# Decode attention's score and value products put into one stretch per round, the exponentials' transposition ahead of it

## The chip, the cores and the metric

The kernel runs on one core of one Trainium2 chip. The metric is the device time of one execution in microseconds (us). Engines are named as in the profile: PE is TensorE (PEld its weight loads), DVE is VectorE, ACT is ScalarE, POOL is GpSimd, SP is SyncE, which only issues transfers.

## What is computed

One inference step of a hybrid decoder layer, in float32. A prompt of 2048 new tokens and 64 sample tokens (8 sequences of 8 tokens) pass through the same layer; only the sample tokens have a cache of 8192 old tokens per sequence, in pages of 128 tokens.

```python
def diff_attn(q, k, v, q_pos, k_pos, lam):
    s = jnp.einsum('bqhcd,bkhcd->bchqk', q, k, preferred_element_type=jnp.float32) * (D_HEAD ** -0.5)
    dist = q_pos[:, None] - k_pos[None, :]
    bias = -alibi_slopes()[:, None, None] * dist.astype(jnp.float32)[None]
    s = jnp.where((dist >= 0)[None, None, None], s + bias[None, None], NEG)
    p = jax.nn.softmax(s, axis=-1)
    a = p[:, 0] - lam * p[:, 1]
    return jnp.einsum('bhqk,bkhd->bqhd', a.astype(v.dtype), v)

def sample_attention(q, k, v, lam, k_pool, v_pool, page_table):
    ...
    kp = k_pool[page_table].reshape(bd, past, N_HEADS, 2, D_HEAD)
    vp = v_pool[page_table].reshape(bd, past, N_HEADS, D_V)
    k_all = jnp.concatenate([kp.astype(k.dtype), k], axis=1)
    v_all = jnp.concatenate([vp.astype(v.dtype), v], axis=1)
    return diff_attn(q, k_all, v_all, past + jnp.arange(tn), jnp.arange(past + tn), lam)

def block_forward(x, conv_state, attend, ...):
    h = rmsnorm(x, norm1_g)
    b, c, u, q, k, v = project(h, w_in)
    y_conv, new_conv = short_conv(b, c, u, conv_state, conv_w)
    o = rmsnorm(attend(q, k, v, lam), subln_g) * (1.0 - lam_init)
    x = x + jnp.concatenate([y_conv, o], axis=-1) @ w_out
    h2 = rmsnorm(x, norm2_g)
    x = x + jnp.square(jax.nn.relu(h2 @ w_up)) @ w_down
```

There are 4 heads, 2 maps per head, 64 numbers per key and 128 per value. "The decode" below is `sample_attention`; the rest (projections, prompt attention, MLP) is "the dense work".

## The kernel before

The dense work is one long stream of products on PE: input projection, prompt attention, output projection and MLP. Each dense product is split into three (`wh`, `wl` are the high and low part of a weight tile; ACT makes `wh`, DVE makes `wl`), and its moving side is 384 or 512 columns wide.

The decode is a generator, `decode()`, with an inner generator `rounds()`. After every dense group of three products `tick(us)` adds to a credit; when the credit is positive and at least `gap * gs` us (by the kernel's own estimates) have gone by since the last step, the generator runs to its next `yield cost, gap`. So the decode's instructions are strewn among the dense ones at fixed places, decided when the program is made; every engine then runs its own list in order. `gp()` gives the gaps, `GP` for the first two sequences and `GP2` for the others, and `gs` is 0.7.

A round takes 1024 cached tokens of a sequence (a pair of chunks of four pages). A sequence has 8 rounds of scores, and its values come 8 rounds later. So a full round has the scores of sequence b and the values of sequence b-1. There are 64 rounds of scores and 64 of values; 48 rounds have both, 16 only scores, 16 only values. The first two sequences run during the input projection, and the other six after the prompt attention, during the output projection and the MLP. A full round does, in this order:

- Scores (line 902): 16 products `sps<-kt,qbd`, in two halves of 8 (one per map), with a `yield` behind each half. Four heads use four column groups of the array, 32 columns of weights each (column tiling). A float32 product is two instructions in the trace. DVE then adds the bias and takes maxima (line 910).
- Some of the next round's transposed keys on DVE: `more(MO[0])`, that is 5 of 8 transposes (`transpose_k`, line 717), then 2 and 1. After the 4th and the 8th, `gather_k` on POOL fetches another chunk's keys (line 699, 128 rows of 8 KB, `kraw`).
- Exponentials (line 858, ACT) that the next round's values need.
- Transposition of this round's exponentials on PE (`pps`, line 937, 4 full-array products) and their copy by ACT to `ptt` (line 940).
- Values (line 949): two halves `e` of 16 products `o_ps<-vpg,ptt`, 16 columns of weights in each of four column groups, with a `yield` behind each half. A half takes its `vpg` tile, four groups `g` of 128 tokens. Behind each half `gather_v` issues four gathers on POOL (line 707, 128 rows of 2 KB each) for the same half of the next round. There are two `vpg` buffers, so a half's buffer is filled again only when its products are done.

Dense sums have 5 of the 8 PSUM banks, the decode 3. A "stretch" below is an unbroken run of column-tiled products on PE with dense products ahead and behind. The last round of a sequence has some more work (new tokens, normalisation) and dense products around it.

Of the kernel before, what the change touches and what calls it, by code (L numbers as in the profile page):

```python
# [8 lines left out]
F32 = mybir.dt.float32  # L9
# [9 lines left out]
P = 128  # L19
# [47 lines left out]
def tile_hymba_step(  # L67
# [68 lines left out]
    def rsqrt(y, v, n, w, eng=None):  # L136
        """y[:n, :w] = v ** -0.5 by Newton's iteration from the exponent trick."""
# [38 lines left out]
    def between(us):  # L176
        """A place between two products where other work of the tensor engine may go."""
        if fillers:
            fillers.pop(0)()
        else:  # L180
            tick(us)
# [15 lines left out]
    def mm3(ps, wh, wl, ah, al, first, last):  # L197
        """ps += (wh + wl)^T (ah + al), all but the product of the two low parts."""
        nc.tensor.matmul(ps, lhsT=wh, rhs=ah, start=first, stop=False)  # L199
        nc.tensor.matmul(ps, lhsT=wh, rhs=al, start=False, stop=False)  # L200
        nc.tensor.matmul(ps, lhsT=wl, rhs=ah, start=False, stop=last)  # L201

    class Weights:
        """Streams [128, 1024] weight tiles and splits each into two float32r parts, ahead of use."""
# [29 lines left out]
        def parts(self):  # L234
            """Closures that split the next tile, a half at a time."""
# [26 lines left out]
        def ahead(self, n):  # L262
            """Splits the next n tiles after those taken."""
            self.split(self.ng + n)
# [6 lines left out]
    def norm_sum(x, n, junk=None):  # L271
        """The mean square of each row of x[:n]."""
# [6 lines left out]
    def norm_root(ss, n, eng=None):  # L279
        """(ss + EPS) ** -0.5 for one value a row."""  # L280
# [23 lines left out]
    # order of the column groups of w_in: Q, K, V, then (C, U, B) per convolution group  # L304
# [5 lines left out]
    # the last block ends with Q, whose results leave without a transpose  # L310
# [4 lines left out]
    # token tiles of each block in two chunks of columns: (source, first row, rows, column)  # L315
# [28 lines left out]
    def prep_sum(bi, ci, ss, i):  # L344
        """Sums of squares of a tile of tokens."""
        x, n = xt[bi, ci][i], chunks[bi][ci][i][2]
        junk = sb.tile([P, D], BF16, tag="nat", bufs=4, name="junk")
        nc.scalar.activation(junk[:n], x[:n], AF.Square, scale=1.0 / 32.0, accum_out=ss[:n, i:i + 1])
# [14 lines left out]
    def prep_scale(bi, ci, rr):  # L363
        """Closures that normalise a chunk's tokens."""
# [7 lines left out]
    def trans(bi, ci):  # L372
        """Closures that transpose and split a chunk's tokens."""
# [29 lines left out]
    # the first tile's norm by itself  # L403
# [42 lines left out]
    class Proj:  # L446
        """One column group of w_in for one block of tokens."""
# [163 lines left out]
    def proj2(bi, mi):  # L611
        """Two column groups, chunk by chunk: at the ends of a block, where the activations change."""
# [58 lines left out]
    def row_fold(dst, src, op):  # L671
        """dst[(h,g,q), c] = over g: op of src[(h,g,q), c]."""
# [10 lines left out]
    def decode():  # L683
# [28 lines left out]
        def transpose_k(r, t, k):  # L712
            """An eighth of the transposed keys of a pair of chunks."""
# [11 lines left out]
        def load_qc(j):  # L725
            """Queries of four batches."""
# [13 lines left out]
        # page rows: keys in rows of 32 groups of four tokens, values token by token  # L740
# [9 lines left out]
        # bias of a cached key: slope (key - end of its pair of chunks) + slope (that end - query)  # L750
# [31 lines left out]
        # a page's scores and values have token 4 s + j in row 32 j + s  # L782
# [3 lines left out]
        # rows of the scores: (head, page in the group of four, token of the sample)  # L786
# [13 lines left out]
        # lambda on every partition  # L800
# [6 lines left out]
        # rows of the output: (head, map, token) in the first 16 of each 32  # L807
# [7 lines left out]
        # new tokens: column s of group g is token 32 g + s = (batch 4 g + s // 8, s % 8)  # L815
        # distance t - q; allowed where it is not positive
        nc.vector.tensor_scalar(scr[:, 0, :], scr[:, 0, :], rowf[:, 0:1], None, op0=ALU.subtract)
        # owner batch of the column, for this row's group
# [17 lines left out]
        # collects rows (h, c, q) into columns (h, q)  # L836
# [13 lines left out]
        def exps(b, k):  # L850
            """Exponentials of a batch's eighth k of the cached keys; NPR: of the new keys."""
# [8 lines left out]
        def more(n):  # L860
            """Some more of the next pair's transposed keys."""
# [6 lines left out]
        def rounds():  # L868
            """The pairs of chunks of batches b0 to b1."""
# [14 lines left out]
            for r in range(b0 * NPR, N_PR + NPR):  # L884
                b, i = divmod(r, NPR)
                pb = b - 1 if b > b0 else -1
                nk = 0
                if r < N_PR:
# [7 lines left out]
                    # scores of this pair of chunks of four pages  # L896
                    sps = dps.tile([P, 2, 256], F32, tag="sps", bufs=DPB - 1, name="sps")
                    for c in range(2):
# [9 lines left out]
                        yield 1.05, gp()[0] if c else gp()[1]  # L908
                    for c in range(2):
                        nc.vector.tensor_tensor_reduce(  # L910
                            sq[:, c, :], sps[:, c, :], base.rearrange("p e j s -> p (e j s)"), 1.0, -3e38,
                            op0=ALU.add, op1=ALU.max, accum_out=cur["mx"][:, c, i:i + 1])
                    if i == NPR - 1 and r + 1 < N_PR:
# [4 lines left out]
                more(MO[0])  # L918
                if pb >= 0:
                    u = st[pb]  # L920
                    if i < NPR - 1:
                        exps(pb, i + 1)
                    else:
                        m2 = small.tile([P, 2], F32, tag="m2", name="m2")
                        nc.vector.tensor_reduce(m2, u["sm"], axis=AX.X, op=ALU.add)
                        sv = small.tile([P, 2], F32, tag="sv", name="sv")
                        row_fold(sv, m2, ALU.add)
                        nc.vector.reciprocal(sv, sv)
                        wr = dk.tile([P, 1], F32, tag="wr", bufs=2, name="wr")
                        nc.vector.tensor_tensor_reduce(sv, sv, osel, 1.0, 0.0, op0=ALU.mult, op1=ALU.add, accum_out=wr)  # L930
                        u["w"] = wr
                    yield 0.0, gp()[2]
                    more(MO[1])
                    pps = dps.tile([P, 2, 2, P], F32, tag="sps", bufs=DPB - 1, name="pps")
                    for e in range(2):
                        for c in range(2):
                            nc.tensor.transpose(pps[:, e, c, :], u["s"][i][:, c, P * e:P * e + P], ident)
                    ptt = dk.tile([P, 2, 16, 2, 8], F32, tag="ptt", name="ptt")
                    for e in range(2):
                        nc.scalar.copy(ptt[:, e].rearrange("p x c q -> p c x q"),  # L940
                                       pps[:, e].rearrange("p c (x q) -> p c x q", q=8))
                    more(MO[2])
                    yield 0.4, gp()[3]
                    for e in range(2):
# [12 lines left out]
                        more(MO[3 + e])  # L957
                        yield 1.2, gp()[4 + e]
                else:
                    for _ in range(3):  # L960
                        yield 0.0, gp()[6]
                        more(2)
                    yield 0.0, gp()[7]
# [75 lines left out]
        # sub-norm of the sample tokens: sums over the partitions by a product with ones  # L1039
# [59 lines left out]
    # units in groups of about four chunks of keys  # L1099
# [9 lines left out]
    # loads by the iteration after which they are issued  # L1109
# [11 lines left out]
    def attention_first():  # L1121
        """The attention's first tiles, ahead of the input projection's end."""
# [7 lines left out]
        # key - query position for the last query block; masked past the diagonal  # L1130
# [36 lines left out]
    def mlp_weights(nxt):  # L1167
        """In order of use; those of the next tokens' output projection come before the last ones."""
# [19 lines left out]
    class Dense:  # L1188
        """Output projection, MLP and final norm of some tokens.

        groups: lists of tiles (source, result, first row, rows); each group of tiles is one chunk of columns.
        """
# [65 lines left out]
        def turn(self, ti, g):  # L1258
            """Transposes and splits half of a tile's normalised tokens."""
# [12 lines left out]
        def norm_early(self, ti, ss):  # L1272
            """Closures for a tile whose group's products go on; all but two tiles of a group wait for its end."""
# [18 lines left out]
        def product(self, ps, ti, w, k2, ks=None):  # L1292
            """Adds the products of a pair of rows of chunks of w_out."""
# [9 lines left out]
        def out_proj(self):  # L1303
# [18 lines left out]
            for half in range(2):  # L1322
                # the first tiles share each pair of rows of weights as it comes
# [58 lines left out]
        def first_ups(self):  # L1382
            """The first ones, group by group: the last group's activations are still being made."""
# [15 lines left out]
        def down(self, ms, after=None):  # L1399
# [26 lines left out]
            if after is not None:  # L1426
                # the result of the last tile, by halves
# [12 lines left out]
        def final(self, ti, eng, last_too=0):  # L1440
            """Final norm: the statistics of tile ti, the result of the tile before it."""
# [11 lines left out]
        def run(self, ub, poll, before_last, nxt, after):  # L1453
# [11 lines left out]
            if len(self.groups) == 1 and KUP:  # L1465
                # the last ones together, half by half of the rows: the memory then takes other tokens' data
# [685 lines left out]
```

## Time and profile before

| | |
|---|---|
| median of three runs | 3152.28 us (3148.69 to 3154.98) |
| profiled execution, first to last instruction | 3153.6 us |
| PE busy / DVE / ACT / POOL | 96% / 58% / 39% / 28% of the span |
| first stage with decode (input projection) | about 110 to 590 us |
| second stage with decode (output projection, MLP) | about 1240 to 2220 us |

A row of the timeline gives the start, the time from the first start to the last end, the engine, the line, and what is written from what; `x16` means that 16 instructions of one kind stand together. Matmuls overlap, so the pace is read from one start to the next. A bracket gives the engine's idle time before the row, and who ended it.

### The profile page before, as it was taken

The page shows a single profiled execution, that of the slowest core. Times are in us where ns is not written, and L with a number is a line of the kernel's source. Part 1 is how long each engine was busy: PE and PEld are TensorE (multiplying, and loading weights), DVE is VectorE, ACT ScalarE, POOL GpSimd, SP SyncE. Part 2 cuts the span into 40 slices and gives each one's busy share as a digit, 9 for nine tenths or more (in the row PEclk, how much of TensorE's full clock was granted, in tenths as well). Part 3 has the DMA queues.
Part 4 walks back from the last instruction along what each step waited for, and adds up shares of the span by engine and source line. Part 5 has one row for each costly group of instructions (what it writes and reads, how often), then busy time and mean ns, then how long its engine had stood idle before and what let it go on. Part 6 is the DMA issues. An engine that isn't in the chain of part 4 may idle for free. (4 is left out here: it accounts for less than half of the span.)

```text
span 3153.6 us, 53285 instructions
## 1 busy us (share of the span) xinstructions
PE 3014.2 (96%) x20902; PEld 2532.3 (80%) x20902; DVE 1824.8 (58%) x3751; ACT 1243.3 (39%) x2705; POOL 891.8 (28%) x1266
## 2 busy tenths in 40 slices
PE   7999998999999989999999999999999999999998
PEld 7988887989997788777677777777887788888886
DVE  5376353268888668766676776663653444444444
ACT  3323323357778643333343333343332332222222
POOL 0013355211122121455466564467002010000002
PEclk9999999999999999999999999999999999999999
DMA  4777876754335457899689899677741112111111
GB/s 149 229 232 247 286 255 200 223 140 113 108 99 146 139 176 242 278 320 334 229 288 360 304 347 328 211 274 263 230 145 41 61 54 67 47 54 47 54 47 64
DMA packets 400821, 585.80 MB, mean 186 GB/s; under 512 B 35413, under 2 KB 299605, under 8 KB 384186
## 3 DMA queue, kind: packets, MB, share of 16 engines
q1 hardware_dynamic: 337418, 301.07, 31.1%
q0 software_dynamic: 61984, 277.91, 24.5%
q8 instruction: 165, 2.70, 0.3%
q10 hardware_dynamic: 1168, 3.41, 0.3%
q14 instruction: 86, 0.70, 0.1%
HBM read 526.56 MB, written 55.74 MB: 185 GB/s over the span
## 5 line engine op out<-in xcount | busy, mean ns | idle before, releaser
L707 POOL DMA_INDIRECT vpg<-in_cache_v_dram,pt x512 | 537.5, 1050 | 232.3 <-issue 134.4
L226 ACT CAST wh<-wraw 128x1024 fp32r<-128x1024 f32 x336 | 350.0, 1048 | 632.2 <-PE dps L1412 277.1
L228 DVE TENSOR_TENSOR wl<-wraw,wh 128x1024 fp32r<-128x1024 f32 x336 | 410.2, 1221 | 236.4 <-ACT wh L226 227.4
L199 PE MATMUL ups<-h2h,wh 128*128 128x384 f32 (+2 forms) x1264 | 462.6, 366 | 4.9 <-DVE x L1417 2.5
L1417 DVE TENSOR_TENSOR x<-dps,x 128x512 f32<-128x512 f32 (+1 forms) x528 | 355.2, 684 | 177.2 <-PE dps L1412 176.7
L1410 PE MATMUL dps<-wh,uh 128*128 128x512 f32 (+1 forms) x1076 | 438.8, 408 | 13.2 <-ACT wh L226 5.6
L201 PE MATMUL ups<-h2h,wl 128*128 128x384 f32 (+2 forms) x1264 | 448.8, 355 | 0.0
L200 PE MATMUL ups<-h2l,wh 128*128 128x384 f32 (+2 forms) x1264 | 447.9, 354 | 0.0
L1411 PE MATMUL dps<-wl,uh 128*128 128x512 f32 (+1 forms) x1076 | 425.5, 395 | 4.3 <-DVE wl L228 3.3
L1412 PE MATMUL dps<-wh,ul 128*128 128x512 f32 (+1 forms) x1076 | 424.2, 394 | 0.0
L199 PE MATMUL ps<-hh,wh 128*128 128x384 f32 (+1 forms) x1152 | 404.6, 351 | 1.1 <-ACT cc L1526 0.7
L201 PE MATMUL ps<-hh,wl 128*128 128x384 f32 (+1 forms) x1152 | 376.5, 327 | 3.1 <-DVE wl L228 3.1
L200 PE MATMUL ps<-hl,wh 128*128 128x384 f32 (+1 forms) x1152 | 376.0, 326 | 0.1
L1369 DVE TENSOR_TENSOR ul<-r,uh 128x384 fp32r<-128x384 f32 (+2 forms) x158 | 93.6, 592 | 438.5 <-ACT uh L1368 438.3
L717 DVE STREAM_TRANSPOSE kt<-kraw 128x512 f32<-128x512 f32 x512 | 316.9, 678 | 5.4 <-DMA kraw<-in_cache_k_dram,idxk 5.4
L699 POOL DMA_INDIRECT kraw<-in_cache_k_dram,idxk x128 | 129.1, 1009 | 565.6 <-DVE kt L717 522.8
L199 PEld LDWEIGHTS ups<-h2h,wh 128*128 128x128 f32 x1264 | 238.5, 189 | 54.4 <-issue 28.7
L1410 PEld LDWEIGHTS dps<-wh,uh 128*128 128x128 f32 (+1 forms) x1076 | 200.8, 187 | 85.8 <-issue 24.1
L1366 ACT ACTIVATE r<-ups 128x384 f32<-128x384 f32 (+2 forms) x158 | 82.8, 524 | 445.0 <-PE ups L201 445.0
L200 PEld LDWEIGHTS ups<-h2l,wh 128*128 128x128 f32 x1264 | 238.9, 189 | 16.6
L201 PEld LDWEIGHTS ups<-h2h,wl 128*128 128x128 f32 x1264 | 238.5, 189 | 15.3
L284 POOL TENSOR_SCALAR ss<-ss 128x1 f32<-128x1 f32 (+1 forms) x33 | 9.5, 289 | 839.5 <-ACT junk L276 838.7
(275 smaller groups left out, 4985.8 us busy)
## 6 DMA issues: line engine op xcount, KB each, us to landing
wraw<-in_w_up_dram SPq DMA_DIRECT2D x128, 512.0 KB, 5.0
wraw<-in_w_down_dram SPq DMA_DIRECT2D x128, 512.0 KB, 3.3
wraw<-in_w_in_dram SPq DMA_DIRECT2D x72, 512.0 KB, 4.4
wraw<-in_w_out_dram SPq DMA_DIRECT2D x32, 512.0 KB, 4.2
x<-in_x_prompt_dram SPq DMA_DIRECT2D x24, 512.0 KB, 7.0
vpg<-in_cache_v_dram,pt POOLq DMA_INDIRECT x512
qt<-QH SPq DMA_DIRECT2D x64, 128.0 KB, 4.5
qt<-QL SPq DMA_DIRECT2D x64, 128.0 KB, 5.0
```

Of the source, the lines that this page charges most:

```text
L199: nc.tensor.matmul(ps, lhsT=wh, rhs=ah, start=first, stop=False)
L200: nc.tensor.matmul(ps, lhsT=wh, rhs=al, start=False, stop=False)
L201: nc.tensor.matmul(ps, lhsT=wl, rhs=ah, start=False, stop=last)
L226: nc.scalar.copy(wh, t)
L228: eng.tensor_sub(wl, t, wh.bitcast(F32))
L699: nc.gpsimd.indirect_dma_start(out=t.rearrange("p a b -> p (a b)"), out_offset=None, in_=ck, in_offset=bass.IndirectOffsetOnAxis(ap=idxk[: ...
L707: nc.gpsimd.indirect_dma_start(out=t[:, g, :], out_offset=None, in_=cv, in_offset=bass.IndirectOffsetOnAxis(ap=idxv[:, 4 * it + g:4 * it + ...
L717: nc.vector.transpose(t[:, e, 16 * j:16 * j + 16].rearrange("p a b -> p (a b)"), kraw[2 * r + e][:, 16 * j:16 * j + 16].rearrange("p a b - ...
L1410: nc.tensor.matmul(ps, lhsT=uh, rhs=wh[:, half], start=(i == 0), stop=False)
L1411: nc.tensor.matmul(ps, lhsT=uh, rhs=wl[:, half], start=False, stop=False)
L1412: nc.tensor.matmul(ps, lhsT=ul, rhs=wh[:, half], start=False, stop=(i == len(ms) - 1))
L1417: nc.vector.tensor_add(xx, ps, xx)
```

## The change

In `rounds()`, the transposition `pps` and the copies to `ptt` come first in a round, with a `yield` behind them. Then both halves of the scores and both halves of the values are issued without a `yield` between, with all eight gathers of the next values behind their halves; then the first five transposed keys, and one `yield` with the summed cost and the gap `gp()[0] + gp()[1]`. The exponentials for the next round come after that, with two more transposed keys, a `yield` with gap `gp()[2] + gp()[4]`, and the last transposed key. The sum of a full round's gaps falls from 12 to 10 (`GP2`), its `yield`s from six to three. Comments were taken out elsewhere.

```diff
                 nk = 0
+                if pb >= 0:
+                    u = st[pb]
+                    pps = dps.tile([P, 2, 2, P], F32, tag="sps", bufs=DPB - 1, name="pps")
+                    for e in range(2):
+                        for c in range(2):
+                            nc.tensor.transpose(pps[:, e, c, :], u["s"][i][:, c, P * e:P * e + P], ident)
+                    ptt = dk.tile([P, 2, 16, 2, 8], F32, tag="ptt", name="ptt")
+                    for e in range(2):
+                        nc.scalar.copy(ptt[:, e].rearrange("p x c q -> p c x q"),
+                                       pps[:, e].rearrange("p c (x q) -> p c x q", q=8))
+                    yield 0.4, gp()[3]
+                cost = 0.0
                 if r < N_PR:
...
-                        yield 1.05, gp()[0] if c else gp()[1]
                     for c in range(2):
                         nc.vector.tensor_tensor_reduce(
...
+                    cost += 2.1
...
+                if pb >= 0:
+                    for e in range(2):
+                        it = NCH * pb + 2 * i + e
+                        v = vpg.pop(it)
+                        for g in range(4):
+                            for h in range(H):
+                                nc.tensor.matmul(
+                                    o_ps[32 * h:32 * h + 16, :],
...
+                        if it + 2 < b1 * NCH:
+                            gather_v(it + 2)
+                    cost += 2.4
                 more(MO[0])
+                yield cost, gp()[0] + gp()[1]
                 if pb >= 0:
-                    u = st[pb]
                     if i < NPR - 1:
                         exps(pb, i + 1)
...
-                    yield 0.0, gp()[2]
                     more(MO[1])
...
+                    yield 0.0, gp()[2] + gp()[4]
                     more(MO[2])
-                    yield 0.4, gp()[3]
-                    for e in range(2):
...
-                        more(MO[3 + e])
-                        yield 1.2, gp()[4 + e]
                 else:
                     for _ in range(3):
-                        yield 0.0, gp()[6]
                         more(2)
-                    yield 0.0, gp()[7]
+                        yield 0.0, gp()[6]
```

The list of PE in a full round of the MLP stage before, from one transposition to the first dense products behind the second half of the scores (`ups` and `dps` are dense sums):

```order
L937 MATMUL pps<-ident,sq 128x128 x4
...
L949 MATMUL o_ps<-vpg,ptt 16x128 x16
L1410 MATMUL dps<-wh,uh 128x512
...
L949 MATMUL o_ps<-vpg,ptt 16x128 x16
L1410 MATMUL dps<-wh,uh 128x512
...
L902 MATMUL sps<-kt,qbd 32x256 x8
L1410 MATMUL dps<-wh,uh 128x512
...
L902 MATMUL sps<-kt,qbd 32x256 x8
L1410 MATMUL dps<-wh,uh 128x512
```

From this transposition to the next there are 57 dense products, 9 of them between the two halves of the values. The same place in the program after, the lines now 893 (`pps`), 914 (scores) and 937 (values):

```order
L893 MATMUL pps<-ident,sq 128x128 x4
L1413 MATMUL dps<-wh,uh 128x512
...
L1415 MATMUL dps<-wh,ul 128x512
L914 MATMUL sps<-kt,qbd 32x256 x16
L937 MATMUL o_ps<-vpg,ptt 16x128 x32
L1413 MATMUL dps<-wh,uh 128x512
```

The four stretches have become one, with 12 dense products between the transposition and the stretch and 30 from the stretch to the next transposition. Over the whole program the runs of score or value products with dense products between fall from 256 to 80. No dense product is added or removed.

On ACT the same place after reads as follows (`wh<-wraw` is a cast of a weight tile that came by a transfer):

```order
L896 COPY ptt<-pps 128x2x16x8 x2
L226 CAST wh<-wraw 128x1024
L858 ACTIVATE sq,sm<-sq,no 128x256 x2
L226 CAST wh<-wraw 128x1024
L896 COPY ptt<-pps 128x2x16x8 x2
```

The exponentials `sq` of line 858 are read by the transposition whose copy is the last row here; before the change a whole round lay between the two.

## Rows read from the trace of the kernel before

**Rows 1.** The page: busy time and share of each engine, whole span.

```profile
PE 3014.2 (96%) x20902; PEld 2532.3 (80%) x20902; DVE 1824.8 (58%) x3751; ACT 1243.3 (39%) x2705; POOL 891.8 (28%) x1266
```

**Rows 2.** Windows: stretch, length, PE, PEld, DVE, ACT, POOL busy, PEclk, DMA share, GB/s.

```profile
1812.00:1908.00 96.00, 96.00 (x927) 73.87 (x926) 69.48 (x119) 36.78 (x73) 65.25 (x61) 1.00 0.98 351
```

**Rows 3.** Timeline of PE, parts of two full rounds.

```profile
1826.57 0.60 PE L937 MATMUL pps<-ident,sq 128*128 128x128 f32 x4
1826.93 0.48 PE L1410 MATMUL dps<-wh,uh 128*128 128x512 f32 x1
1827.24 0.39 PE L1411 MATMUL dps<-wl,uh 128*128 128x512 f32 x1
...
1829.31 0.39 PE L1411 MATMUL dps<-wl,uh 128*128 128x512 f32 x1
1829.53 0.39 PE L1412 MATMUL dps<-wh,ul 128*128 128x512 f32 x1
1829.85 1.07 PE L949 MATMUL o_ps<-vpg,ptt 128*16 128x128 f32 x32
1830.85 0.50 PE L1410 MATMUL dps<-wh,uh 128*128 128x512 f32 x1
1831.19 0.40 PE L1411 MATMUL dps<-wl,uh 128*128 128x512 f32 x1
...
1838.55 0.34 PE L201 MATMUL ups<-h2h,wl 128*128 128x384 f32 x1
1838.82 1.07 PE L902 MATMUL sps<-kt,qbd 128*32 128x256 f32 x16
1839.82 0.44 PE L199 MATMUL ups<-h2h,wh 128*128 128x384 f32 x1
1840.10 0.34 PE L200 MATMUL ups<-h2l,wh 128*128 128x384 f32 x1
1840.27 0.34 PE L201 MATMUL ups<-h2h,wl 128*128 128x384 f32 x1
```

**Rows 4.** Timeline within that score stretch: its last eight, its last four instructions.

```profile
1839.27 0.61 PE L902 MATMUL sps<-kt,qbd 128*32 128x256 f32 x8
1839.49 0.40 PE L902 MATMUL sps<-kt,qbd 128*32 128x256 f32 x4
```

**Rows 5.** Line 937 in 1811:1910, then in 2117:2206 (values only): count, ns, first and last start.

```profile
L937 PE MATMUL pps<-ident,sq x28: 271/272/273, 1811.6 to 1908.7; 128*128 128x128 f32 x28
...
L937 PE MATMUL pps<-ident,sq x32: 271/272/273, 2118.7 to 2204.7; 128*128 128x128 f32 x32
```

**Rows 6.** POOL's groups in 1812:1908, the last in 1600:1800: count, busy us, mean ns.

```profile
L707 POOL DMA_INDIRECT vpg<-in_cache_v_dram,pt x48 | 52.4, 1092 | 14.6 <-issue 12.2 <-DMA vpg<-in_cache_v_dram,pt 1.2 <-PE dps L1412 0.6
L699 POOL DMA_INDIRECT kraw<-in_cache_k_dram,idxk x12 | 12.6, 1047 | 17.3 <-DVE kt L717 16.1 <-issue 0.9 <-DVE ul L1369 0.3
...
L289 POOL TENSOR_SCALAR ss<-ss 128x1 f32<-128x1 f32 x9 | 7.3, 813 | 1.4 <-DVE ss L287 0.8
```

**Rows 7.** Timelines of PE and POOL, 2148 to 2165: a half of values, three gathers, the wait.

```profile
2148.02 1.07 PE L949 MATMUL o_ps<-vpg,ptt 128*16 128x128 f32 x32
...
2149.39 0.94 POOL L707 DMA_INDIRECT vpg<-in_cache_v_dram,pt  x1 [4.16 <-PE o_ps L949]
...
2159.04 1.89 POOL L707 DMA_INDIRECT vpg<-in_cache_v_dram,pt  x1 [0.30 <-issue]
...
2164.21 0.41 PE L949 MATMUL o_ps<-vpg,ptt 128*16 128x128 f32 x8 [1.58 <-DMA vpg<-in_cache_v_dram,pt]
```

**Rows 8.** PE's waits over the whole span: total us, times, longest.

```profile
PE o_ps L949 <- DMA vpg<-in_cache_v_dram,pt: 20.7, 25, 2.3
...
PE o_ps L949 <- ACT ptt L940: 13.3, 6, 5.0
```

**Rows 9.** Windows around a wait for `vpg`: columns as in group 2.

```profile
2196.00:2200.00 4.00, 2.02 (x36) 1.02 (x35) 0.00 (x0) 0.00 (x0) 3.05 (x4) 1.00 0.98 324
2200.00:2203.50 3.50, 3.50 (x14) 3.50 (x13) 0.48 (x1) 2.04 (x4) 2.62 (x3) 0.53 0.64 224
```

More of the change, by code (lines that the diff above doesn't have):

```diff
@@ L917, in rounds @@
                         gather_v(b0 * NCH + 1)
-                more(MO[0])
                 if pb >= 0:
-                    u = st[pb]
[L921 to L931, printed above, removed]
-                    yield 0.0, gp()[2]
-                    more(MO[1])
-                    pps = dps.tile([P, 2, 2, P], F32, tag="sps", bufs=DPB - 1, name="pps")
-                    for e in range(2):
[L936 to L942, printed above, removed]
-                    yield 0.4, gp()[3]
                     for e in range(2):
@@ L956, in rounds @@
                             gather_v(it + 2)
-                        more(MO[3 + e])
-                        yield 1.2, gp()[4 + e]
+                    cost += 2.4
+                more(MO[0])
+                yield cost, gp()[0] + gp()[1]
+                if pb >= 0:
+                    if i < NPR - 1:
+                        exps(pb, i + 1)
+                    else:
+                        m2 = small.tile([P, 2], F32, tag="m2", name="m2")
+                        nc.vector.tensor_reduce(m2, u["sm"], axis=AX.X, op=ALU.add)
+                        sv = small.tile([P, 2], F32, tag="sv", name="sv")
+                        row_fold(sv, m2, ALU.add)
+                        nc.vector.reciprocal(sv, sv)
+                        wr = dk.tile([P, 1], F32, tag="wr", bufs=2, name="wr")
+                        nc.vector.tensor_tensor_reduce(sv, sv, osel, 1.0, 0.0, op0=ALU.mult, op1=ALU.add, accum_out=wr)
+                        u["w"] = wr
+                    more(MO[1])
+                    yield 0.0, gp()[2] + gp()[4]
+                    more(MO[2])
                 else:
                     for _ in range(3):
+                        more(2)
                         yield 0.0, gp()[6]
-                        more(2)
-                    yield 0.0, gp()[7]
                 if pb >= 0 and i == NPR - 1:
```

## Prediction

> **What bounds the kernel now.** I read the busy line first: PE is busy 96% of the span, no other engine over 58% [rows 1]. So time falls by what PE is spared, unless a new wait takes it back. The window 1812 to 1908 us, with six full rounds, shows what else is near its end there [rows 2]: PE has no idle time in 96.00 us, the DMA share is 0.98 at 351 GB/s, and POOL, whose busy time leaves out the gaps between its issues, is at 65 of 96 us. Rounds stand 16.2 us apart, (1908.7 - 1811.6) / 6 [rows 5]. So in this stage PE is the bound, with DMA and POOL close behind.
>
> **What the change removes.** The timeline gives a stretch's price by comparing starts with the dense pace. Dense products of 512 columns start about 0.23 us apart, those of 384 about 0.17. From the last dense start ahead of a half of the scores to the second one behind it are 1840.10 - 1838.55 = 1.55 us, 1.21 more than two paces; a half of the values costs 1831.19 - 1829.53 - 0.46 = 1.20 [rows 3]. Within a score stretch a group of four column tiles starts every 0.22 us [rows 4], so four groups need 0.88 and the other 0.33 us is entering and leaving the stretch. Values are half as wide, eight groups at half the distance: the same. The order has 256 stretches before and 80 after, so 176 x 0.33 = 58 us go. The step from scores to values inside the new stretch is not in the trace; it costs 0 to 0.33 us in 48 rounds, 0 to 16 us. I take 0, since the groups within a stretch show no break when the head or the weights change. The transpositions cost 0.44 us (1827.24 - 1826.57 - 0.23) before and after, and no product is added.
>
> **What the change moves, PE.** Rounds come closer, since the summed gaps are shorter. In the order after, a full round has 42 dense products where it had 57: 18 of 384 columns and 24 of 512 make 8.6 us, the transpositions 0.44, the stretch 4 x 0.87 + 0.33 = 3.8, together 12.8 us. Worked out so for all, 36 full rounds have an own length of 12.3 to 13.5 us, mean 12.6, and 13 rounds of values alone 10.6 to 12.1, mean 11.3; the others lie further apart (ends of sequences, other dense work in between) and are not in danger. What has to fit into a round besides is unchanged: ten gathers on POOL, 4.2 MB of keys and values (two times 1 MB and eight times 256 KB).
>
> **POOL.** In the window of group 6 six rounds have 48 value gathers of 1.09 us and 12 key gathers of 1.05, and each is followed by a gap of 0.30 us [rows 6, 7]: (52.4 + 12.6 + 60 x 0.30) / 6 = 13.8 us a round. That fitted into 16.2 us, and POOL even waited 16.1 us in the window for transposed keys. It does not fit into 12.6. From 1600 to 1800, some twelve rounds long, POOL has norm work as well, the largest group alone 7.3 us [rows 6]; for this I add 0.6 us a round. So short full rounds take 14.4 us, and PE waits 36 x (14.4 - 12.6) = 65 us.
>
> **The value gathers' chain.** A half's buffer is refilled only behind its own products. A half starts at 2148.02, its first gather at 2149.39, 1.37 us later. A last gather started at 2159.04 lasted 1.89, and PE's fourth group was released at 2164.21, 3.28 us after the gather's end [rows 7]. After the change both halves stand back to back, so eight gathers follow the first half: 1.37 + 8 x 1.39 - 0.30 + 3.28 = 15.5 us until the second half's fourth group may go, which stands 0.87 + 0.65 = 1.5 us into the next round's values. The rounds must be 13.9 us apart (12.8 with undisturbed gathers of 0.95). Before, nine dense products of 0.17 us and another entry lay between the halves, 1.9 us more time for the late half: 12.0, and the trace has (2204.7 - 2118.7) / 7 = 12.3 us in the stage with values alone [rows 5]. So the formula holds. In full rounds POOL's 14.4 covers this; in rounds of values alone PE waits 13 x (13.9 - 11.3) = 34 us. The present waits for `vpg`, 20.7 us [rows 8], are replaced by these.
>
> **What I cost at nothing.** The exponentials are now needed about 3 us (a gap of 4 x 0.7) after their place instead of a round later, behind weight casts on ACT that themselves await transfers; PE's transposition would wait, with all dense products behind it. In return the copies to `ptt` have the scores' 1.75 us as extra cover; PE waits 13.3 us for them now [rows 8]. I take the two as even, -13 to +13. The key gathers stand behind eight value gathers in POOL's list, so keys land later and DVE, which transposes them, holds up sums behind it. DVE is busy 69 of 96 us [rows 2] and dense sums have five banks; without that cover it is perhaps 1 us in 36 rounds, but within a round that waits for POOL anyway. The rounds of scores alone only lose a stretch (counted); their moved key transposes lie under the dense work.
>
> **Sum.** -58 + 65 + 34 - 21 = +20 us. The profiled execution has a span of 3153.6 us against a median of 3152.3, so the sum carries over: 3172 us, 0.6% more.
>
> **The rivals.**
>
> *The gathers keep up (faster).* If POOL's gathers take their undisturbed 0.95 + 0.30 us, ten take 12.5 and with the norm work 13.1; full rounds wait 36 x 0.5 = 18 us, values alone 13 x (12.8 - 11.3) = 20, and the sum is -58 + 38 - 21 = -41: 3111 us. For it: the shorter gathers shown took 0.94 [rows 7]. Against it: the mean in the densest window is 1.09, and denser rounds would not lower it. It decides from short full rounds of under 13.9 us, where the sum is zero.
>
> *DMA is the bound.* A round of 16.2 us at 351 GB/s is 5.7 MB; with 42 instead of 57 dense products' weights 5.3 MB remain, 15.1 us at that rate, and the share was 0.98 [rows 2]. Full rounds then wait 36 x 2.5 = 90 us: +45, 3197 us. Against it: PE did not wait at this share. The Trainium skill ("DMA: Bandwidth & Descriptors", "Where 436 GB/s comes from") puts the HBM limit of a core at about 358 GB/s; by that a round would take 14.8 us and the time be 3186 us, and the window's 351 GB/s agrees with it.
>
> *The clock falls.* Behind a wait of nearly 2 us for `vpg`, PE was granted 0.53 of its clock for 3.5 us (its level of 1.2 GHz), where it had 1.00 before [rows 9]: 1.6 us lost. If every second of the 49 waits brings this and it adds to the sum, it is 24 x 1.6 = 39 us: 3211 us. Against it: POOL works on meanwhile, so a slower PE mostly shortens the next wait. The Trainium skill ("TensorE: Matmul & The Clock Gate", "HAM oscillation — how this bites in real kernels") tells of a kernel that falls to the lower clock at each wait for a transfer; these rows agree that a wait can do it.
>
> **How the numbers follow.** My forecast (rounds of 13.9 to 14.9 us, 3154 to 3190) has 0.53, the gathers that keep up 0.23, DMA 0.14, the clock 0.10. Changes within 0.2%, 6 us, can hardly be told from none: of my forecast's chance 0.14 lies there and 0.03 below. Faster 0.26, same 0.14, slower 0.60. The range 3112 to 3212 reaches from the second case, half of which it leaves out, to the fourth; it holds the unknown 16 and 13 us.
>
> **What the profile after would show.** Stretches of about 3.8 us, and PE's instructions otherwise unchanged: the 58 us. PE's wait for `vpg` from 20.7 to about 100 us, at the last groups of the second half. Short full rounds 14 to 15 us apart, with POOL's issues nearly without a pause; rounds of values alone about 14. Wrong if short rounds come at 13 us (then faster), if PE waits for weights (DMA), for `sq` or for `kt`, or if the granted clock falls under 0.95 between 1300 and 2200 us.

## The result, and the profile after

The changed kernel takes 3264.56 us (median of four runs, 3255.69 to 3270.32) where the kernel before takes 3153.35 beside it: 1.0356 times as long, 95% interval 1.0335 to 1.0378, 111 us more. The direction was forecast, the size was not: 3172 us, and 3212 as the end of the range.

The page of the changed kernel (lines 893 `pps`, 896 `ptt`, 914 scores, 937 values, 699 and 707 the gathers, 717 the key transposes): the busy line, and the chain that ended last.

```profile
PE 3001.7 (92%) x20902; PEld 2594.0 (80%) x20902; DVE 1821.5 (56%) x3751; ACT 1245.0 (38%) x2705; POOL 890.8 (27%) x1266
...
PE 52%; DMA 16%; issue 13%; DVE 8%; POOL 8%; ACT 3%; SPq 0%; POOLq 0%; ACTq 0%; DVEq 0%
DMA kraw<-in_cache_k_dram,idxk 7%; DMA vpg<-in_cache_v_dram,pt 6%; PE ups L199 5%; PE ups L201 5%; PE ups L200 5%; PE dps L1414 5%; PE dps L1415 5%; PE dps L1413 5%; POOL vpg L707 5%; PE asc L1835 4%; PE O L1922 3%; PE ps L199 3%; PE ps L201 3%; PE ps L200 3%; DVE kt L717 2%
...
L717 DVE STREAM_TRANSPOSE kt<-kraw 128x512 f32<-128x512 f32 x512 | 326.9, 684 | 184.9 <-DMA kraw<-in_cache_k_dram,idxk 184.4
```

PE is busy only 12.5 us less than in [rows 1], and not because little was saved. Its mean granted clock fell from 0.986 to 0.968 over the span. The clock has two levels in these traces, full and half. Before, it was at half for 86 us, and PE was busy in 77 of them; after, for 206 us, with PE busy in 163. Counting a busy us at half clock as half a us of work, the clock costs half of that busy time: 38 us before, 81 after. Time in which PE was idle at half clock is idle time only. Busy time less this loss is the work, and span less busy time is the idle time. All pairs below are split like this:

| | span | work | idle | lost to the clock |
|---|---|---|---|---|
| before | 3153.6 | 2976 | 139 | 38 |
| after | 3253.8 | 2920 | 252 | 81 |
| difference | +100 | -55 | +113 | +43 |

PE's waits over the span, the counterpart of [rows 8] (total us, times, longest):

```profile
PE sps L914 <- DVE kt L717: 60.7, 31, 5.0
PE o_ps L937 <- DMA vpg<-in_cache_v_dram,pt: 41.3, 40, 3.1
PE ops L986 <- DVE osc L983: 16.1, 6, 5.8
...
PE o_ps L978 <- ACT pttn L974: 11.3, 1, 11.3
...
PE pps L893 <- ACT sq L858: 9.9, 6, 8.4
```

The largest wait is the scores' for the transposed keys `kt`. The same wait before, and DVE's own wait for `kraw` before, which is 184.4 us above:

```profile
PE sps L902 <- DVE kt L717: 1.7, 2, 0.9
DVE kt L717 <- DMA kraw<-in_cache_k_dram,idxk: 5.4, 4, 2.9
```

The window of [rows 2], and the transpositions of one sequence's eight full rounds:

```profile
1812.00:1908.00 96.00, 79.58 (x793) 65.30 (x791) 66.02 (x128) 28.67 (x57) 56.97 (x58) 0.91 0.95 344
```

```profile
L893 PE MATMUL pps<-ident,sq x32: 271/272/273, 1303.6 to 1409.9; 128*128 128x128 f32 x32
```

In the window PE, which had no idle time, now has 16.4 us; the clock is 0.91, and DMA moves hardly less. The rounds stand (1409.9 - 1303.6 - 0.4) / 7 = 15.1 us apart: 16.2 before, 12.6 by the products alone, 14.4 forecast.

One such wait in full, from the timelines of POOL, DVE and PE, and the window behind it:

```profile
1508.84 2.49 DVE L717 STREAM_TRANSPOSE kt<-kraw 128x512 f32<-128x512 f32 x4
1509.46 0.96 POOL L707 DMA_INDIRECT vpg<-in_cache_v_dram,pt  x1 [3.90 <-PE o_ps L937]
...
1518.28 0.95 POOL L707 DMA_INDIRECT vpg<-in_cache_v_dram,pt  x1 [0.31 <-issue]
1519.53 1.84 POOL L699 DMA_INDIRECT kraw<-in_cache_k_dram,idxk  x1 [0.30 <-DVE x L1420]
1521.68 0.95 POOL L699 DMA_INDIRECT kraw<-in_cache_k_dram,idxk  x1 [0.30 <-issue]
1522.93 0.96 POOL L707 DMA_INDIRECT vpg<-in_cache_v_dram,pt  x1 [0.30 <-DMA vpg<-in_cache_v_dram,pt]
...
1528.60 3.12 DVE L717 STREAM_TRANSPOSE kt<-kraw 128x512 f32<-128x512 f32 x5 [6.74 <-DMA kraw<-in_cache_k_dram,idxk]
...
1535.13 0.70 DVE L717 STREAM_TRANSPOSE kt<-kraw 128x512 f32<-128x512 f32 x1
...
1535.98 3.44 PE L914 MATMUL sps<-kt,qbd 128*32 128x256 f32 x32 [4.11 <-DVE kt L717]
```

```profile
1536.00:1539.50 3.50, 3.50 (x44) 1.98 (x48) 0.95 (x2) 0.00 (x0) 1.66 (x1) 0.56 0.71 238
```

Read it downwards. The fourth transposed key is done at 1511.33, and with it a key buffer is free. The key gather for it comes to its turn only at 1519.53, behind eight value gathers; POOL has had only its usual gap of 0.30 us. Its data are there at 1528.60, 9 us later; until then DVE stands still for 6.74 us, with dense sums queued behind. The eighth transpose is done at 1535.8, and the scores start 4.11 us late. Then the clock is 0.56 for 3.5 us, and the scores, two halves of 0.87 us by the prediction, take 3.25, to the values' start at 1539.23.

### The profile page after: what moved, and what is told of

It reads as the page before. It is cut to its first block, busy times and chain, and to the rows that moved or that the text cites. A ratio compares the mean times of both kernels' runs of the same rounds, so it can differ in the third digit from the quotient of the medians.

```text
span 3253.8 us, 53325 instructions
## 1 busy us (share of the span) xinstructions
PE 3001.7 (92%) x20902; PEld 2594.0 (80%) x20902; DVE 1821.5 (56%) x3751; ACT 1245.0 (38%) x2705; POOL 890.8 (27%) x1266
## 4 chain that ended last, share of the span: by engine, by line
PE 52%; DMA 16%; issue 13%; DVE 8%; POOL 8%; ACT 3%; SPq 0%; POOLq 0%; ACTq 0%; DVEq 0%
DMA kraw<-in_cache_k_dram,idxk 7%; DMA vpg<-in_cache_v_dram,pt 6%; PE ups L199 5%; PE ups L201 5%; PE ups L200 5%; PE dps L1414 5%; PE dps L1415 5%; PE dps L1413 5%; POOL vpg L707 5%; PE asc L1835 4%; PE O L1922 3%; PE ps L199 3%; PE ps L201 3%; PE ps L200 3%; DVE kt L717 2%
## 5 line engine op out<-in xcount | busy, mean ns | idle before, releaser
L707 POOL DMA_INDIRECT vpg<-in_cache_v_dram,pt x512 | 518.3, 1012 | 385.0 <-PE o_ps L937 240.1
L1413 PE MATMUL dps<-wh,uh 128*128 128x512 f32 (+1 forms) x1076 | 432.7, 402 | 13.3 <-ACT wh L226 7.1
L717 DVE STREAM_TRANSPOSE kt<-kraw 128x512 f32<-128x512 f32 x512 | 326.9, 684 | 184.9 <-DMA kraw<-in_cache_k_dram,idxk 184.4
L1414 PEld LDWEIGHTS dps<-wl,uh 128*128 128x128 f32 (+1 forms) x1076 | 201.8, 188 | 58.4 <-DVE wl L228 15.7
```

Source lines behind the costliest of these rows:

```text
L707: nc.gpsimd.indirect_dma_start(out=t[:, g, :], out_offset=None, in_=cv, in_offset=bass.IndirectOffsetOnAxis(ap=idxv[:, 4 * it + g:4 * it + ...
L717: nc.vector.transpose(t[:, e, 16 * j:16 * j + 16].rearrange("p a b -> p (a b)"), kraw[2 * r + e][:, 16 * j:16 * j + 16].rearrange("p a b - ...
L1413: nc.tensor.matmul(ps, lhsT=uh, rhs=wh[:, half], start=(i == 0), stop=False)
L1414: nc.tensor.matmul(ps, lhsT=uh, rhs=wl[:, half], start=False, stop=False)
```

## The theories

**Chains**: rounds of 12.6 us are shorter than what the gathers need, keys first, since they stand behind eight value gathers, then values; the clock falls behind the waits. **Full queue**: POOL's ten issues a round are the limit, and late keys only follow. **Long stretch**: holding PE for nearly 4 us hurts by itself, whatever the spacing. Bytes as the limit (the DMA rival) came up again with the trace after.

Runs made together form a set, and each set had its own runs of the kernel before. In the sets marked † it took 3250 to 3271 us instead of 3150, so ratios and differences within a set are used there. In the † traces with all gathers 65 to 75 us of PE's waits have no releaser on record (none in the other sets), so the waits named there are lower bounds.

## Experiments on the spacing

**gap_wide**† (changed kernel, wider gaps everywhere):

```diff
-                yield cost, gp()[0] + gp()[1]
+                yield cost, gp()[0] + gp()[1] + 2
-                    yield 0.0, gp()[2] + gp()[4]
+                    yield 0.0, gp()[2] + gp()[4] + 2
```

> The changed kernel with the gap behind the stretch and the one behind the exponentials each 2 larger: by the order a full round's own length on PE goes from about 12.6 to 15.6 us, a round of values alone from 11 to 14; still one stretch a round. Chain theory (the rounds became shorter than the gathers' chains, keys first of all): the waits for kt and vpg fall from 61 and 41 us to under 15 each, the clock recovers, and the removed 58 us show: 3100 +- 20 us. Long-stretch theory (the loss comes from holding PE for 3.8 us at once, whatever the spacing): over 3200 us.

**two_stretches**† (before, with `yield 2.1, gp()[0] + gp()[1]` behind both halves of the scores, and `yield 2.4, gp()[4] + gp()[5]` behind both halves of the values):

> The kernel before with the pause inside the scores and the one inside the values taken out, their gaps and costs added up: 128 stretches instead of 256, transposition where it was, key gathers where they were. Both theories: 128 x 0.33 = 42 us of PE work go. Chain theory: own rounds of 14.9 us leave the chains room, only the rounds of values alone (own length about 10) wait more, 20 us or so: 3130 +- 15 us. Long-stretch theory: stretches of about 2 us cost half of what the change cost, no gain: 3160 or more.

**shorter_rounds**† (before, with its four stretches):

```diff
-GP2 = (2, 1, 2, 3, 2, 2, 3, 3)
+GP2 = (1, 1, 1, 2, 1, 1, 3, 3)
```

> The kernel before with its four stretches, only the gaps of the last six sequences smaller (1, 1, 1, 2, 1, 1, sum 7), so that full rounds in the order are 11.9 to 14.0 us long, mean about 12.9 (before about 16.2, after 12.6). Chain theory (rounds shorter than the gathers' chains): as slow as after or slower, ratio 1.03 to 1.05, with waits of PE for vpg of 40 us or more and few for kt, since here each key gather stands behind four value gathers at most; half clock as long as in after. Long-stretch theory (holding PE for 3.8 us at once is what costs): ratio under 1.015, half clock near that of before.

**after_again**† (the changed kernel beside it):

> The changed kernel itself, beside other variants on one chip, as the measure for them. Every theory: a ratio of about 1.035 to the kernel before (1.030 to 1.040), PE waits for kt of about 60 us, DVE waits for kraw of about 180 us.

Measured: gap_wide 1.0238 (1.0189 to 1.0288), two_stretches 1.0218 (1.0166 to 1.0270), shorter_rounds 1.0285 (1.0233 to 1.0337), after_again 1.0322 (1.0275 to 1.0370). So closer rounds without any merging cost nearly what the change costs: spacing is a cause by itself. And shorter_rounds does it with few waits for `kt`, as expected:

```profile
PE o_ps L949 <- ACT ptt L940: 55.0, 17, 8.3
...
PE o_ps L949 <- DMA vpg<-in_cache_v_dram,pt: 34.8, 34, 3.2
...
PE sps L902 <- DVE kt L717: 9.7, 10, 2.1
```

after_again waits 38.2 us for `kt` (60 expected) and DVE 68.3 for `kraw` (180 expected). gap_wide and two_stretches did not come out as the chain theory said; gap_wide still waits 50.7 us for `kt`, where under 15 was expected. They are not clean, though: their rounds are 15.6 and 14.9 us long by the order, still under 16.2, and in these sets gathers cost more (below).

In sets with the kernel before at 3150 us, the wide rounds in the last six sequences alone:

**gap_late3** (both gaps above with `+ (3 if b0 else 0)`):

> The changed kernel with 6 more in the gaps of a full round of the last six sequences, so that rounds are 16.6 to 17.3 us long in the order (before 16.2, after 12.6) and rounds of values alone 15; the first two sequences stay as in the changed kernel. Spacing alone as the cause: ratio 0.99 to 1.005. The burst of eight gathers with keys behind it as the cause, whatever the spacing: ratio 1.015 to 1.03, waits for kt still 30 us or more.

**second_00** (`rounds()` of before for the first two sequences, that of the change for the others), and **second_22** (the same, with `+ 2` in both gaps):

```diff
-            yield from rounds()
+            yield from (rounds() if b0 else rounds_first())
```

> The first two sequences in the order of before, the last six as in the changed kernel (rounds of 12.6 us). If the change costs in each stage what the milestones of the traces say, some 22 us of the 111 go and about 80 stay: ratio 1.022 to 1.030, waits for kt 50 us or more. If the first stage's delay carries nothing over: the same as the changed kernel, 1.035.

> The first two sequences in the order of before, the last six in the changed order with 4 more in the gaps of a full round, so that rounds are 15.2 to 16.6 us long in the order and the decode ends at the same place among the dense products as before. Spacing as the cause, with the saved stretches as gain: 10 to 25 us less than before (ratio 0.992 to 0.997), waits for kt under 25 us. The late keys and the burst as a cause beside spacing: 0 to 20 us more than before.

Measured: gap_late3 1.0174 (1.0147 to 1.0201), second_00 1.0283 (1.0260 to 1.0306), second_22 1.0077 (1.0053 to 1.0101). The first stage thus has 22 of the 111 us (111 - 89), as the start of the prompt attention's scores says, at 643.5 us before and at 664.2 after, in this row of the changed kernel:

```profile
L1835 PE MATMUL asc<-kst,qt x640: 274/393/775, 664.2 to 1118.0; 128*128 128x512 f32 x112, 128*128 128x256 f32 x32, 128*128 128x384 f32 x16
```

By the ratios, with rounds about as long as before 65 of second_00's 89 us go; the other 24 stay, where spacing alone was to give 10 to 25 us less than the kernel before. gap_late3 (55 us slower) has besides the first stage a single wait of 27.7 us for a weight at 2350 us: the decode ends late there, the next tokens' loads are issued behind its end, and the weight's load stands behind them in SP's list.

## Experiments on the gathers

**no_keys**† (the changed kernel) and later **before_nokeys**† and **second_nokeys**† (before and second_22):

```diff
-                kraw.pop(2 * r + e)
-                if 2 * r + e + 2 < b1 * NCH:
-                    gather_k(2 * r + e + 2)
+                kraw[2 * r + e + 2] = kraw.pop(2 * r + e)
```

> The changed kernel without the fetch of cached keys after the first two chunks of each stage (the old keys are transposed again and again): 112 or so key gathers and their 1 MB each are left out. Key theory: the wait for kt goes to nearly nothing, what is left is the value chain, waits for vpg 40 to 90 us: 3150 +- 25 us. If the value chain and the clock alone made the loss, the time stays over 3220.

**before_free**† and **after_free**† (the edit above, and `vpg[it + 2] = v` for `gather_v(it + 2)`):

> The kernel before without its gathers after the first two chunks of keys and of values of each stage (the products take the first ones again; left out: all later key and value gathers). Every theory: less than before by the waits for vpg of 20.7 us and the clock behind them, ratio about 0.98 to 0.99. It is the measure for the next run.

> The changed kernel with the same gathers left out. Chain theory and full-queue theory: no gather, no wait for kt beyond some us, and the saved stretches show: 40 to 58 us less than the kernel before without gathers, ratio about 0.965. Long-stretch theory: no gain over it, ratio 0.98 to 1.01, with PE waiting for weights, for ACT and DVE, and a low clock nonetheless.

**before_half** and **after_half**, with **before_again** beside them:

```diff
-                out=t.rearrange("p a b -> p (a b)"), out_offset=None, in_=ck,
+                out=t[:, 0:32].rearrange("p a b -> p (a b)"), out_offset=None, in_=ck2,
-                    out=t[:, g, :], out_offset=None, in_=cv,
+                    out=t[:, g, 0:2 * P], out_offset=None, in_=cv2,
```

> The kernel before with every gather moving half of its bytes (128 rows of 4 KB for keys, of 1 KB for values) with as many gather instructions and all waits in place; left out: the other half of the keys and values, in whose place the products take the first half again. POOL's issues as the limit: within 20 us of the kernel before (3250). Bytes as the limit (the queues are full behind the burst): 3100 to 3150.

> The changed kernel with the same half of the bytes left out. Ten gathers a round still take POOL 12.6 us or more. POOL's issues as the limit: still slower than the kernel before with half of the bytes, by 60 to 100 us, waits for kt and vpg hardly less (50 us together). Bytes as the limit: faster than that kernel by about 20 us (as without gathers), waits for kt and vpg under 20 us.

> The kernel before, for a trace of it on the chip of the variants, where its median was 3270 us. Every theory: about 3270 us; against the kernel before without gathers (3083 us) it shows what the gathers cost there, and in which waits; half clock between the 88 us of the first trace and the 290 us of the changed kernel.

Measured: before_free 0.9431 (0.9379 to 0.9484), after_free 0.9360 (0.9307 to 0.9412), 3085.0 and 3061.5 us. The gathers cost the kernel before more than the 1 to 2% expected. Without them the change makes the kernel 23 us faster (40 to 58 was expected), so a long stretch by itself does not make it slower. The 34 full rounds of the second stage that are under 22 us apart in either kernel average 12.8 us there and 15.3 in the changed kernel: it is the gathers that hold them apart. Its waits for `kt` are 3.8 us. The busy lines of the two, with clocks of 0.992 and 0.986 and spans of 3082.8 and 3060.3:

```profile
PE 2986.9 (97%) x20902; PEld 2523.4 (82%) x20902; DVE 1821.4 (59%) x3751; ACT 1242.4 (40%) x2705; POOL 248.9 (8%) x646
```

```profile
PE 2940.8 (96%) x20902; PEld 2561.7 (84%) x20902; DVE 1821.7 (60%) x3751; ACT 1243.3 (41%) x2705; POOL 251.4 (8%) x646
```

By the same split (PE busy in 40 of 49 us at half clock, and in 72 of 87) work falls by 62 us, and idle time (+24) and clock (+16) take back 40 of it, even with no gather in the way.

With half of the bytes: before_half 0.9877 (0.9843 to 0.9911), after_half 1.0087 (1.0059 to 1.0114), 3113 and 3179 us: the change costs 66 us where it costs 111 with all bytes, beside a kernel before of the same time. Half of the bytes make 45 of the difference; the other 66 us remain with as many issues a round, their chains and the other half of the bytes. after_half still waits like this:

```profile
PE sps L916 <- DVE kt L719: 40.4, 24, 3.2
PE o_ps L939 <- DMA vpg<-in_cache_v_dram,pt: 31.0, 23, 4.3
```

before_again gave 3153.5 us in that set and tells only that the trace of before repeats (PE 3013.7 us busy). The comparison of gather costs in the slower sets, for which it was meant, is had from the ratios: there all gathers cost the kernel before 186 us (3271.0 - 3085.0), the changed one 312.

no_keys took 3270 us in its one run, the time of the kernel before in its set (3269), but its waits for `kt` are still 38.5 us, with no key gather at all. So late keys are not the only way in which `kt` comes late. And the kernel before without key gathers takes 0.974 of its own time (before_nokeys, below): by these two ratios, from different sets and one of a single run, the change costs some 2.7% without any key gather, of 3.2 to 3.6 with them.

**keys_between**† (the changed kernel, the second half's four value gathers behind the first five transposes, so that POOL has a key gather in between) and **second_keys** (the same edit in second_22):

```diff
-                        if it + 2 < b1 * NCH:
+                        if e == 0 and it + 2 < b1 * NCH:
                             gather_v(it + 2)
                 more(MO[0])
+                if pb >= 0 and it + 2 < b1 * NCH:
+                    gather_v(it + 2)
```

> The changed kernel, but the four value gathers of the second half are issued behind the first five key transposes, so that a key gather stands between the two groups of four in POOL's list instead of behind all eight. Key theory (keys land too late because eight value gathers stand ahead of them): the first key gather goes about 5 us earlier, PE's wait for kt falls from 61 to under 25 us and the time by 30 us or more, to 3235 or less. Full-queue theory (POOL's ten gathers a round are the limit, the keys' lateness only follows from it): same number of gathers, the waits move from kt to vpg, time within 15 us of the changed kernel's.

> As second_22, but the second half's four value gathers are issued behind the first five transposed keys, so that a key gather stands ahead of them in POOL's list. Late keys as a cause: waits for kt fall under 10 us, DVE's wait for kraw under 30 us, and the time is 5 to 20 us under that of second_22. POOL's list as the limit (what keys win, values lose): the same time within 10 us, waits for vpg 20 us more.

Measured: 1.0337 (1.0298 to 1.0375) and 1.0094 (1.0067 to 1.0121), no better than without the edit. keys_between still waits 44.9 us for `kt`. In second_keys waits for `kt` fall from 29.1 to 22.1 us and those for `vpg` in the merged stretch rise from 3.9 to 25.9: what the keys win, the values lose. With buffers for one round ahead, the order in POOL's list only chooses who waits.

## What is left at wide spacing

second_22 has 44 us less work than before by the split (busy 2983.0 of 3175.8 us, clock 0.982), but 53 us more idle time and 13 more lost to the clock. Its waits for `kt` and for `wl`:

```profile
PE sps L1073 <- DVE kt L717: 29.1, 14, 4.9
PE dps L1573 <- DVE wl L228: 25.1, 15, 5.4
```

Some of these waits are of another kind. In the changed kernel 28 of the 31 waits for `kt`, with 58.7 us of the 60.7, have a wait of DVE for `kraw` that ended in the 9 us ahead of the scores. Here it is 3 of 14, with 2.1 us; but in the 14 us ahead, since the rounds are longer, it is 11 of 14, with 22.3 us. So late keys may have a share here too. What holds DVE in one of the three with no such wait, from its timeline, and PE's row:

```profile
1506.11 1.23 DVE L228 TENSOR_TENSOR wl<-wraw,wh 128x1024 fp32r<-128x1024 f32 x1 [3.77 <-ACT wh L226]
1507.26 0.70 DVE L717 STREAM_TRANSPOSE kt<-kraw 128x512 f32<-128x512 f32 x1
...
1508.11 2.67 PE L1073 MATMUL sps<-kt,qbd 128*32 128x256 f32 x32 [2.72 <-DVE kt L717]
```

The last transposed key stands behind a weight's `wl`, which awaits ACT. In the code before, gaps of 3, 2 and 2 and the value products lie between that key and the scores; in the changed code a gap of 3, 2.1 us. A delay of DVE that the old place covered now reaches PE.

> The kernel before without its key gathers after the first two chunks of each stage (the products take the first keys again; left out: all later key gathers); value gathers unchanged. The measure for the next run: 3100 to 3140 us where the kernel before takes 3150.

> second_22 with the same key gathers left out. Late keys behind eight value gathers as what is left at wide spacing: 15 to 25 us less than the kernel before without key gathers, waits for kt under 10 us, waits for wl back to about 5 us. The burst of eight value gathers itself, or PE's spared time turning into waits for other engines: the same time within 10 us or more.

Measured: 0.9737 (0.9683 to 0.9791) and 0.9784 (0.9732 to 0.9836). The intervals overlap, and the gain that the theory of late keys asked for is not there; `kt` is waited for 44.8 us, in 26 waits, with no key gather. That fits the key's place. To put that key earlier was not tried, so its share stays open.

**scores_one** (before, only the two halves of the scores in one stretch, gathers untouched):

```diff
-                        yield 1.05, gp()[0] if c else gp()[1]
+                    yield 2.1, gp()[0] + gp()[1] + 1
```

> The kernel before with only the two halves of the scores in one stretch (64 stretches fewer) and one more in the gap, so that rounds are as far apart as before (15.2 to 16.7 us). Gathers, values and their order are unchanged. If a saved stretch gives 0.33 us: 21 us less than before (ratio 0.993). If it gives what the kernels without gathers showed, 23 of 58: 8 us less (ratio 0.9975). If a longer stretch costs by itself: 10 us more or worse.

Measured: 1.0028 (1.0015 to 1.0040), 9 us slower by the ratio. Its page has PE busy for 2990.9 us of 3155.1 at a clock of 0.986, the clock of before: by the split (busy in 69 of 89 us at half clock) 19 us less work, 64 x 0.33 = 21 was expected, 25 us more idle time and 4 less lost to the clock. With the gathers in place no version of the merged stretch beat the kernel before.

## Why the prediction was wrong in size

Of the theories the chains stand in their main part: rounds shorter than the gathers of keys and values need cost most of it. 58.7 us of waits at `kt` stand behind DVE's waits for keys, but how much time late keys cost beside late values is not shown: shorter_rounds loses nearly as much with few waits for `kt`, and without key gathers most of the loss stays. The full queue is part of the same thing, since keys and values share POOL's list and DMA, and neither issues nor bytes alone explain it. The long stretch as a cause by itself falls with after_free.

- *-58 us for the stretches*: right. Work fell by 55 us in the changed kernel and by 62 without gathers. The step from scores to values cost nothing that shows.
- *"So time falls by what PE is spared, unless a new wait takes it back"*: too simple. scores_one gave back all of its 19 us with no gather moved, the kernels without gathers 40 of 62. Seen from PE at 96%, the other chains (weights through ACT and DVE, sums through DVE) seemed far off; where PE gets faster they are the next to be waited for.
- *Short full rounds held to 14.4 us by POOL*: they are 15.1 us apart. That something holds them was right; at wide spacing 65 us came back. POOL's issues alone are not the holder: half of the bytes with as many issues took 45 us off the difference.
- *Rounds of values alone, 13.9 us*: right on the mean. The last eight rounds' transpositions of the changed kernel, 2045.1 to 2144.4 us, are 14.1 apart, though between 10.9 and 18.5. The waits for `vpg` in the rounds of values alone are 13.4 us in the first stage and 9.5 in the second, where 34 was forecast.
- *Waits for `vpg` of about 100 us*: 41.3. The rest of the waiting stands at `kt`.
- **The step that failed first** is in "what I cost at nothing": key gathers behind eight value gathers as "perhaps 1 us in 36 rounds, but within a round that waits for POOL anyway". The scores waited 60.7 us for `kt`. I had followed the buffer of the values from gather to product, and not that of the keys: issue behind eight gathers, 9 us to landing, eight transposes, one `kt`.
- **The second** is the clock, a rival with 0.10, "POOL works on meanwhile, so a slower PE mostly shortens the next wait". It cost 43 us beside 113 of waiting instead of lying in the waits, the largest single miss of the sum; no run shows how long the waits would have been at full clock. The Trainium skill ("TensorE: Matmul & The Clock Gate", "HAM oscillation — how this bites in real kernels") has the mechanism of that rival; the rows at 1536 us agree.
- *The exponentials and `ptt` as even*: right. The wait for `ptt` fell from 13.3 to 0.2 us, and `pps` waits 9.9 us for `sq`, 8.4 of it once.

In sum: forecast -58 + 65 + 34 - 21 = +20. Measured -55 work, +113 idle, +43 clock, +100 in the profiled runs before rounding: 3 worse in the work, 35 in the waits, 43 in the clock.

## What to carry to other kernels

Shortening the busiest engine's list also moves everything that was issued between its pieces: before pricing it, follow each buffer with a single spare copy from its release through issue, landing and use, and compare that chain with the new distance of rounds. A wait on TensorE is to be priced with the clock behind it, as part of the sum. Split a profile into work, idle time and clock; the busy share alone hid 55 us of real gain.

## What was not expected of the hardware

The same kernel took 3150 us in some sets of runs and 3250 to 3271 in others, while without gathers it took 3085 in one of the latter. It is not a property of the chip alone: the record names chip 12 for a set at 3149 us and for a later one at 3251. The cause stays open. And a gather whose instruction on POOL lasts 1.84 us has its data there 9 us after its start, in a stretch (1520.5 to 1528.6 us) in which DMA was 0.94 busy at 344 GB/s. The Trainium skill ("DMA: Bandwidth & Descriptors", "Issuing engines are not separate DMA queues") says that transfers started by ScalarE, SyncE or GpSimd run on the same 16 DMA engines and interleave; that agrees with keys which land while values and weights go by, but no run separates their shares.
